# First layer's expert 0 gets its tokens by one-hot products from rows in SBUF instead of an indirect gather, and the slot columns are read one job later

## The chip, the core and the metric

One core of a Trainium2 chip runs the whole kernel as one launch. The metric is the device time of that launch in microseconds (us), the median of several executions. TensorE (PE) multiplies matrices, VectorE (DVE) and ScalarE (ACT) work elementwise, GpSimd (POOL) does elementwise work and issues the indirect DMAs, SyncE (SP) issues most of the weight transfers.

## The reference

Two layers run over 256 latent tokens and 256 context tokens of width 1024. Each layer has a mixer and then a mixture of experts (MoE); only the latent stream is returned, so the second layer's MoE sees 256 tokens and the first layer's sees all 512. What matters here is the MoE and what stands ahead of it:

```python
x_lat = x_lat + g1 * hybrid_mixer(p, u, v, q_a, g, keys, lp, rope_tabs)   # ends with "merged @ w_out"
h2 = modulate(rmsnorm(x_lat, norm2_g[l]), sh2, sc2)                       # h * (1 + scale) + shift
x_lat = x_lat + g2 * moe(h2, router_w, router_b, w_e_gate[l], w_e_up[l], w_e_down[l])
...
# moe(t): 16 experts in 4 groups; best group by its two largest scores, then top 2 experts in it
scores = sigmoid(t @ router_w); sel = scores + router_b
...
for e in range(N_EXPERTS):
    a = silu(t @ w_gate[e]) * (t @ w_up[e])          # 1024 -> 512
    y = y + gate[:, e:e + 1] * (a @ w_down[e])       # 512 -> 1024
```

## The kernel before

**Sparse experts.** Each expert gets a fixed number of slots (64 tokens, for some 64 + 32 or more), cut into *jobs* `(expert, first slot, g)`, with `g = 128 / slots`. With g = 2 a job has 64 slots and the two halves of a 1024-wide row lie on two groups of 64 partitions; with g = 4 it has 32 slots and four groups of 32. The first layer has 25 jobs; job 0 is expert 0's first 64 slots, job 1 its next 32, jobs 2 and 3 the same for expert 1, jobs 4 and 5 are experts 2 and 3. Tokens beyond the slots are handled by a loop at the end of the layer.

**Routing.** Token tile by token tile (t = 0 to 3, 128 tokens each) the output projection ends, `decide(t)` computes the row's rms (`rms`), the router logits (`logit`) and the normalised, modulated rows h2 (`h2_out`), which go to DRAM (`h2d`). At t = 3, `pick` runs a long chain of small DVE operations that ends with the choice `mm_` (1 where a token chose an expert); `first_idx` forms every token's rank within its expert (a prefix sum on TensorE, then `rk`), and `order` counts tokens per expert (`cnt`).

**How a job gets its tokens.** An indirect DMA on POOL (`gather`, issued by `pull_job`) reads the job's rows from h2d by a column of indices into one of three buffers `xgb`. `put_x` transposes them on TensorE and ACT copies the result to `ex`; then the gate and up products (L1614) run. For the experts of fixed rank, 0 and 1 (`fixed` holds their four jobs), the index column is made on the spot by `first_list`: a one-hot of the ranks (DVE, L1159), four one-column matmuls against the token numbers (L1163), and a conversion (L1165). For all others `place` writes a slot list to DRAM with eight indirect DMAs (L1212, index `r_ai`), `fetch` reads it back (`lr`, L1447), and `spread` turns it into columns `sel` and `ixh` (DVE L1454, TensorE L1459, DVE L1462 to L1467). In the second layer the tokens of the fixed experts are already picked another way: `dispatch` multiplies one-hots of the ranks with the h2 rows in SBUF.

**Job order.** In job j TensorE runs gate and up, and in between the previous job's transposes (`hidden`, L1592), its down product (`down`, L1547), the next job's `put_x` (L1383), and for pairs of jobs the sum into the latent rows (`add`, L1581). `sel` is needed from the first `down` on, since it scales the result, so `spread` runs in job 1. `blocks` is a chain of small DVE operations about the overflow loop, in program order after job 1.

**Order of the engines.** Each engine runs its own queue strictly in order, so an instruction that waits holds up all behind it. A scheduler fills the queues from the program's order and estimated times. `warm(n)` puts n matmuls into the TensorE queue whose result nobody reads. Weights stream through eight slots of 2 MB (`wx`); SP issues a slot's next transfer (L1261) when its last reader has ended. POOL issues all indirect DMAs; each takes POOL about 1 us.

## Time and profile before

| | us |
|---|---|
| median of 3 runs | 1330.26 (1328.95 to 1332.95) |
| the profiled execution's own time | 1331.49 |
| its span in the trace | 1329.7 |
| TensorE busy in it | 1228.7 |
| first layer's MoE: starts of the first gate product and of the last down product | 525.57 and 809.84 |

Times in the trace count from the start of the span. The trace lists each f32 matmul as two records, so a count "x16" there stands for 8 matmuls of the program. The mean granted TensorE clock over the span was 0.974 of full speed.

### The profile page before, as it was taken

The page shows a single profiled execution, that of the slowest core. Times are in us where ns is not written, and L with a number is a line of the kernel's source. Part 1 is how long each engine was busy: PE and PEld are TensorE (multiplying, and loading weights), DVE is VectorE, ACT ScalarE, POOL GpSimd, SP SyncE. Part 2 cuts the span into 40 slices and gives each one's busy share as a digit, 9 for nine tenths or more (in the row PEclk, how much of TensorE's full clock was granted, in tenths as well). Part 3 has the DMA queues.
Part 4 walks back from the last instruction along what each step waited for, and adds up shares of the span by engine and source line. Part 5 has one row for each costly group of instructions (what it writes and reads, how often), then busy time and mean ns, then how long its engine had stood idle before and what let it go on. Part 6 is the DMA issues. An engine that isn't in the chain of part 4 may idle for free. (4 is left out here: it accounts for less than half of the span.)

```text
span 1329.7 us, 23222 instructions
## 1 busy us (share of the span) xinstructions
PE 1228.7 (92%) x9376; PEld 830.2 (62%) x9376; DVE 613.0 (46%) x1372; ACT 408.0 (31%) x766; POOL 281.4 (21%) x304
## 2 busy tenths in 40 slices
PE   5899989999999998899999997799999999888985
PEld 2587755656777775555555554688988855555543
DVE  4546545456323554522212234837666854434332
ACT  4434234342222310222212333545554410111111
POOL 0424330002111114212112211544601311100000
PEclk9899989999999997999999998899999999999998
DMA  9421566657564938697999845534343789999993
GB/s 381 156 72 60 191 219 210 207 190 248 180 206 156 355 136 314 243 402 299 417 404 416 327 148 189 204 107 146 118 156 122 276 297 396 421 424 422 425 421 119
DMA packets 70718, 338.48 MB, mean 255 GB/s; under 512 B 9506, under 2 KB 21202, under 8 KB 58064
## 3 DMA queue, kind: packets, MB, share of 16 engines
q1 hardware_dynamic: 59328, 320.93, 64.5%
q0 software_dynamic: 4912, 8.27, 1.8%
q10 hardware_dynamic: 6368, 7.76, 1.6%
q8 instruction: 75, 1.23, 0.4%
q14 instruction: 35, 0.29, 0.1%
HBM read 332.64 MB, written 10.02 MB: 258 GB/s over the span
## 5 line engine op out<-in xcount | busy, mean ns | idle before, releaser
L1614 PE MATMUL mmp<-wx,wh 128*64 128x256 f32 (+1 forms) x3456 | 257.0, 329 | 4.9 <-DVE wh L1528 3.4
L1614 PEld LDWEIGHTS mmp<-wx,wh 128*64 128x64 f32 (+1 forms) x3456 | 161.9, 123 | 92.1 <-issue 40.1
L197 PE MATMUL mmp<-xh,wh 128*128 128x512 f32 (+2 forms) x576 | 209.0, 364 | 8.3 <-ACT xh L421 7.5
L199 PE MATMUL mmp<-xh,wl 128*128 128x512 f32 (+2 forms) x576 | 199.4, 347 | 0.0
L1547 PE MATMUL trp<-wx,r 128*32 128x256 f32 (+1 forms) x944 | 129.1, 480 | 9.5 <-DVE r L1594 9.5
L197 PEld LDWEIGHTS mmp<-xh,wh 128*128 128x128 f32 (+1 forms) x576 | 108.3, 189 | 33.3 <-ACT xh L421 8.0
L199 PEld LDWEIGHTS mmp<-xh,wl 128*128 128x128 f32 (+1 forms) x576 | 108.4, 188 | 18.2 <-issue 2.6
L198 PE MATMUL mmp<-xres,wh 128*128 128x512 f32 (+1 forms) x288 | 114.8, 399 | 0.0
L205 ACT CAST wh<-raw 128x1024 fp32r<-128x1024 f32 (+2 forms) x53 | 54.0, 1024 | 127.3 <-PE mmp L198 47.5
L1547 PEld LDWEIGHTS trp<-wx,r 128*32 128x32 f32 (+1 forms) x944 | 44.6, 122 | 74.3 <-issue 53.5
L198 PE MATMUL mmp<-xl,wh 128*128 128x256 f32 (+2 forms) x288 | 85.1, 296 | 5.3 <-DVE xl L382 5.2
L194 DVE TENSOR_TENSOR wl<-raw,wh 128x1024 fp32r<-128x1024 f32 (+2 forms) x43 | 51.6, 1201 | 82.1 <-ACT wh L205 81.8
L1565 DVE TENSOR_TENSOR wl<-r,wl 64x512 fp32r<-64x512 f32 x54 | 37.1, 686 | 96.7 <-ACT wl L1564 78.6
L205 ACT CAST wh<-wx 128x1024 fp32r<-128x1024 f32 (+2 forms) x55 | 55.9, 1025 | 56.8 <-issue 23.6
L1389 POOL DMA_INDIRECT ysd<-r,ixh x25 | 25.1, 1005 | 199.9 <-ACT r L1556 198.9
L1556 ACT ACTIVATE r<-trp,sel 128x512 f32<-128x512 f32 (+1 forms) x25 | 15.5, 619 | 167.7 <-PE trp L1547 167.7
L198 PEld LDWEIGHTS mmp<-xres,wh 128*128 128x128 f32 (+1 forms) x288 | 54.2, 188 | 15.0 <-issue 1.7
L1641 DVE TENSOR_TENSOR r<-r,mmp 128x256 f32<-128x256 f32 (+1 forms) x43 | 15.9, 370 | 102.4 <-ACT r L1640 102.4
L198 PEld LDWEIGHTS mmp<-xl,wh 128*128 128x128 f32 (+1 forms) x288 | 54.5, 189 | 11.5 <-DVE xl L382 5.9
L194 DVE TENSOR_TENSOR wl<-wx,wh 128x1024 fp32r<-128x1024 f32 (+1 forms) x44 | 56.1, 1283 | 8.1 <-ACT wh L205 8.0
L1581 PE MATMUL atp<-wl 128*128 128x512 f32 (+1 forms) x176 | 48.3, 416 | 11.1 <-ACT wl L1568 7.8
L1346 POOL DMA_INDIRECT wh<-h2d,ixh x24 | 28.2, 1173 | 122.0 <-PE trp L1383 90.8
(388 smaller groups left out, 2075.8 us busy)
## 6 DMA issues: line engine op xcount, KB each, us to landing
wx<-in_wexp_dram SPq DMA_DIRECT2D x79, 2048.0 KB
raw<-in_wmod_dram SPq DMA_DIRECT2D x80, 512.0 KB
wx<-in_wexp_dram SPq DMA_DIRECT2D x44, 512.0 KB
raw<-in_win_dram SPq DMA_DIRECT2D x35, 512.0 KB
wx<-in_win_dram SPq DMA_DIRECT2D x35, 512.0 KB
raws<-in_wmod_dram SPq DMA_DIRECT2D x8, 1024.0 KB
xres<-in_wexp_dram SPq DMA_DIRECT2D x5, 1024.0 KB
trk<-in_wexp_dram SPq DMA_DIRECT2D x5, 1024.0 KB
```

Of the source, the lines that this page charges most:

```text
L194: e.tensor_tensor(dst, full, hi.bitcast(F32), op=OP.subtract)
L197: T.matmul(o, lh, rh, start=first, stop=False, skip_group_check=True)
L198: T.matmul(o, lh, rl, start=False, stop=False, skip_group_check=True)
L199: T.matmul(o, ll, rh, start=False, stop=last_, skip_group_check=True)
L205: S.copy(h[:, :n], src)
L1346: return G.indirect_dma_start(out=xg[:, :D // g], out_offset=None, in_=h2d.rearrange("r (h d) -> (r h) d", h=g), in_offset=bass.IndirectOf ...
L1389: s_i = G.indirect_dma_start(out=ysd.rearrange("r (h d) -> (r h) d", h=g), in_=y, in_offset=None, out_offset=bass.IndirectOffsetOnAxis(ap= ...
L1547: T.matmul(py[i * P // g:(i + 1) * P // g, :w], aT[:, (c % m) * P + c // m * (P // g):(c % m) * P + (c // m + 1) * (P // g)], wcols(wd, o, ...
L1565: V.tensor_tensor(hb[1][rs, cs], y2[rs, :w], yh_.bitcast(F32), op=OP.subtract)
L1581: T.matmul(acc[t][h], one[h][rs, t * P:(t + 1) * P], hb[n][rs, h * 512:(h + 1) * 512], start=(j == 1 and n == 0 and not last), stop=(n == ...
L1614: parts(g, lambda h, gs_: mms.append(T.matmul(px[gs_, i * f:(i + 1) * f], ex[:, (k % n) * P + k // n * q:(k % n) * P + (k // n + 1) * q], ...
L1641: misc["a0"] = V.tensor_tensor(a0[:, :f], a0[:, :f], px[:, f:2 * f], op=OP.mult)
```

## The change

In the first layer the two jobs of expert 0 no longer go through an index column and a gather. All four h2 tiles get SBUF rows of their own (`h2s`), so they stay until the ranks are known. `first_idx` builds one-hots for the two jobs, and `dispatch`, now also for g = 4, multiplies them with the h2 rows into PSUM; DVE copies job 0's result and ACT job 1's to `xgb`. The index columns for expert 1's two jobs move from job 0 into `first_idx`. For the last token tile, h2 is no longer made by ACT and two POOL products but by two DVE operations, the first of them placed right behind the residual sum. The six `warm` matmuls behind `order` go. `spread` and the first two `down` products run in job 2 instead of job 1 (`SPR`), and the gathers for jobs 2 and 3 stand ahead of `place` and of job 0.

```diff
-        h2s = [bcx[:, NR + i, :] for i in range(2)]
+        h2s = [bcx[:, (NR + i) % 4, :] for i in range(NT)]
...
             elif t == NT - 1:
-                S.activation(h2, xres[:, t, :], AF.Copy, scale=rss[:, t:t + 1])
-                G.tensor_tensor(h2, h2, a2b[r], op=OP.mult)
-                G.tensor_tensor(h2, h2, sh2[r], op=OP.add)
+                V.scalar_tensor_tensor(h2, h2, rss[:, t:t + 1], sh2[r], op0=OP.mult, op1=OP.add)
...
-            for n in range(len(fixed) if last else 2):
+            if last:
+                for n in range(len(fixed)):
+                    one_hot(n, hot[:, n])
+                return
+            for n, h in [(n, one_hot(n, r2([P, NT, P // fixed[n][2]]))) for n in range(2)]:
+                dispatch(n, h, 1 - n)
+            for n in range(2, len(fixed)):
                 first_list(n)
-        def dispatch(n):
+        def dispatch(n, h, eng):
+            g = fixed[n][2]
             px = trp()
+            w = D // g
             for t in range(NT):
-                halves(lambda i, gs_: T.matmul(px[gs_], hot[:, n, t], h2s[t][:, i * 512:(i + 1) * 512], start=(t == 0),
-                                               stop=(t == NT - 1), skip_group_check=True))
-            (V.tensor_copy if n == 1 else S.copy)(xgb[n], px)
+                for i in range(g):
+                    T.matmul(px[i * P // g:(i + 1) * P // g, :w], h[:, t], h2s[t][:, i * w:(i + 1) * w], start=(t == 0),
+                             stop=(t == NT - 1), skip_group_check=True)
+            (V.tensor_copy if eng else S.copy)(xgb[n][:, :w], px[:, :w])
...
                 order()
-                if not last:
-                    warm(6)
...
                 res = V.tensor_tensor(x_t[:, hs], x_t[:, hs], tm, op=OP.add)
+                if hf and t == NT - 1 and not last:
+                    V.tensor_tensor(h2s[t], x_t, a2b[r], op=OP.mult)
...
-            for v in range(len(fixed), LA + 2):
+            for v in range(len(fixed), LA + SPR + 1):
                 pull_job(v)
+        SPR = 1 if last else 2
...
-            for j in range(2):
-                tc.keep_in_program_order(pull_job(j))
+            tc.keep_in_program_order(pull_job(2))
         place()
...
-        pend = None
+        pend, downs = None, []
+        if not last:
+            tc.keep_in_program_order(pull_job(3))
...
-                    if i == (j == 1) and pend is not None:
-                        if j == 1:
+                    if j >= SPR and i == (j == SPR):
+                        if j == SPR:
                             spread()
-                        down(pend[0], aT, pend[2])
-                    if i == 0 and j == 0 and not last:
-                        for v in range(2, len(fixed)):
-                            first_list(v)
-                        for v in range(2, min(LA + 1, len(fixed))):
-                            pull_job(v)
+                        while downs:
+                            down(*downs.pop(0))
```

What this does to the queues is seen at three places. TensorE in the first layer, from behind the prefix sum to job 0's gate product, before (L1163 index columns, L1175 counts, L1269 warm, L1383 `put_x`, L1614 gate and up):

```order
L1163 MATMUL trp<-cst,r_4144 128x1 x4
L1163 MATMUL trp<-cst,r_4152 128x1 x4
L1175 MATMUL trp<-r_mm,ones 128x16 x4
L1269 MATMUL mmp<-cst,st_69 128x512 x6
L1383 MATMUL trp<-st_69,wh 128x128 x4
L1163 MATMUL trp<-cst,r_4325 128x1 x4
L1163 MATMUL trp<-cst,r_4333 128x1 x4
L1383 MATMUL trp<-st_69,wh 128x128
L1614 MATMUL mmp<-wx_3689,wh 64x256 x16
```

and now the same stretch (lines renumbered: L1152 `dispatch`, L1173 index columns, L1185 counts, L1394 `put_x`, L1627 gate and up):

```order
L1152 MATMUL trp<-xh,r_4148 64x512 x8
L1152 MATMUL trp<-xh,r_4150 32x256 x16
L1173 MATMUL trp<-cst,r_4181 128x1 x4
L1173 MATMUL trp<-cst,r_4189 128x1 x4
L1185 MATMUL trp<-r_mm,ones 128x16 x4
L1394 MATMUL trp<-st_69,wh 128x128 x6
L1627 MATMUL mmp<-wx_3689,wh 64x256 x16
```

24 `dispatch` matmuls have come in ahead of the counts, the six warm matmuls are gone, and `put_x` of both jobs stands ahead of job 0. The second place is POOL's queue from the end of the routing to the first gather by the slot list, before (L1079 and L1080 the two h2 products, L1346 gathers, L1212 slot list writes, L1447 its read):

```order
L1079 TENSOR_TENSOR xh<-xh,bcy 128x1024
L1080 TENSOR_TENSOR xh<-xh,bcy 128x1024
L1346 DMA wh<-h2d_3613,r_ix_3657 128x512
L1346 DMA wh<-h2d_3613,r_ix_3657 128x256
L1212 DMA lst_3621<-tokid,r_ai 9216x4 x8
L1346 DMA xg<-h2d_3613,r_ix_3657 128x512
L1346 DMA wh<-h2d_3613,r_ix_3657 128x256
L1447 DMA lr_4224<-lst_3621 128x64
L1447 DMA lr_4226<-lst_3621 32x64
```

and now (L1360 gathers, here of jobs 2 and 3, L1222 the writes, L1458 the read):

```order
L1360 DMA xg<-h2d_3613,r_ix_3657 128x512
L1360 DMA wh<-h2d_3613,r_ix_3657 128x256
L1222 DMA lst_3621<-tokid,r_ai 9216x4 x8
L1458 DMA lr_4247<-lst_3621 128x64
L1458 DMA lr_4249<-lst_3621 32x64
```

The products are gone, and nothing stands between the list's writes and its read any more; job 3's gather, which waits for job 0's transposes to leave its buffer, stands ahead of the writes. The third place is DVE between the first silu product and the columns, now (L1650 silu product of jobs 0 and 1, L1605 copy of `hidden`, L1465 and L1466 the conversion of the list, the others `blocks`); before, the conversion L1454 stood right behind job 0's silu product and `blocks` behind the columns:

```order
L1650 TENSOR_TENSOR r_4448<-r_4448,mmp 128x128
L1422 TENSOR_TENSOR r_4452<-r_4452,cst 1x256
L1465 CAST lf_4248<-lr_4247 128x16x2
L1466 COPY lf_4248<-lr_4247 128x16
L1423 TENSOR_REDUCE r_4453<-r_4452 1x16
L1465 CAST lf_4250<-lr_4249 32x16x2
L1466 COPY lf_4250<-lr_4249 32x16
L1424 TENSOR_TENSOR r_ov<-r_cnt,r_4453 1x16
```

Here `blocks` stands behind the conversion and ahead of L1605, the copy that job 1's `down` and the PSUM slot of `spread` need.

## Rows read from the trace of the kernel before

**Rows 1.** The page: TensorE's busy time (part 1) and DMA share (part 2).

```profile
PE 1228.7 (92%) x9376; PEld 830.2 (62%) x9376; DVE 613.0 (46%) x1372; ACT 408.0 (31%) x766; POOL 281.4 (21%) x304
...
DMA  9421566657564938697999845534343789999993
```

**Rows 2.** TensorE timeline from the routing to job 0 (start, length, what, count, idle before).

```profile
498.96 5.22 PE L1269 MATMUL mmp<-cst,st 128*128 128x512 f32 x8
...
509.87 3.54 PE L1163 MATMUL trp<-cst,r 128*128 128x1 f32 x16 [1.13 <-DVE r L1159]
513.28 1.87 PE L1175 MATMUL trp<-r_mm,ones 128*128 128x16 f32 x8
514.99 7.52 PE L1269 MATMUL mmp<-cst,st 128*128 128x512 f32 x12
522.35 0.60 PE L1383 MATMUL trp<-st,wh 128*128 128x128 f32 x4
522.78 0.95 PE L1163 MATMUL trp<-cst,r 128*128 128x1 f32 x8
...
525.57 7.09 PE L1614 MATMUL mmp<-wx,wh 128*64 128x256 f32 x48
```

**Rows 3.** Busy time by stretch; the third number from the end is the granted clock.

```profile
502.30:509.00 6.70, 2.92 (x13) 1.54 (x11) 5.28 (x27) 0.63 (x1) 0.00 (x0) 1.00 1.04 396
509.10:519.30 10.20, 9.43 (x29) 6.97 (x30) 5.75 (x22) 0.00 (x0) 2.43 (x2) 0.50 0.70 243
```

**Rows 4.** DVE timeline of the routing and the list's index.

```profile
489.92 1.28 DVE L1082 SCALAR_TENSOR_TENSOR xh<-xres,r_rss,bcy 128x1024 f32<-128x1024 f32 x1 [0.66 <-POOL r_rss L1070]
...
492.38 0.23 DVE L1065 SCALAR_TENSOR_TENSOR r_lgs<-r_lgs,r_rss,r_cr 128x16 f32<-128x16 f32 x1
...
497.59 1.55 DVE L1065 SCALAR_TENSOR_TENSOR r_lgs<-r_lgs,r_rss,r_cr 128x16 f32<-128x16 f32 x1
499.47 2.12 DVE L1106 TENSOR_SCALAR r_sco<-r_sco 128x64 f32<-128x64 f32 x1 [0.32 <-ACT r_sco L1105]
...
507.33 0.23 DVE L1127 TENSOR_TENSOR r_mm<-r_ohs 128x64 f32<-128x64 f32 x1
...
515.18 0.17 DVE L1176 COPY r_cnt<-trp 128x16 f32<-128x16 f32 x1 [1.49 <-PE trp L1175]
...
519.79 0.15 DVE L1209 TENSOR_SCALAR r_ai<-r_af 128x8 int32<-128x8 f32 x1
```

**Rows 5.** POOL timeline: an h2 product, first list write, read of the list.

```profile
496.77 2.34 POOL L1079 TENSOR_TENSOR xh<-xh,bcy 128x1024 f32<-128x1024 f32 x1 [1.26 <-ACT xh L1078]
...
520.22 1.21 POOL L1212 DMA_INDIRECT lst<-tokid,r_ai  x1 [3.37 <-DVE r_ai L1209]
...
534.99 1.14 POOL L1447 DMA_DIRECT2D lr<-lst  x2 [1.95 <-DMA lst<-tokid,r_ai]
```

**Rows 6.** DVE timeline: conversion of the list, then the ends of a piece of `blocks`.

```profile
537.37 0.17 DVE L1454 CAST lf<-lr 128x32 f32<-128x32 int32 x1
...
549.23 0.41 DVE L1412 TENSOR_REDUCE r<-r 1x16 f32<-1x256 f32 x1
...
554.53 0.41 DVE L1426 TENSOR_REDUCE r<-r 1x16 f32<-1x256 f32 x1
```

**Rows 7.** TensorE timeline within the jobs.

```profile
541.13 1.10 PE L1459 MATMUL trp<-lf,st 128*64 128x45 f32 x32
...
555.29 1.93 PE L1547 MATMUL trp<-wx,r 128*32 128x256 f32 x32 [2.15 <-DVE r L1594]
...
558.07 1.50 PE L1614 MATMUL mmp<-wx,wh 128*32 128x128 f32 x42 [0.48 <-ACT wh L1521]
...
581.68 1.95 PE L1614 MATMUL mmp<-wx,wh 128*64 128x256 f32 x16
...
597.30 3.60 PE L1547 MATMUL trp<-wx,r 128*64 128x512 f32 x16
```

**Rows 8.** The longest of SP's waits from 530 to 760 us (total, times, longest).

```profile
SPq L1261 <- PE mmp L1614: 121.4, 22, 19.6
```

More of the change, by code (lines that the diff above doesn't have):

```diff
@@ L1073, in h2_out @@
             r = t // 2
-            h2 = h2s[t % 2]
+            h2 = h2s[t]
             if last:
@@ L1138, in first_idx, with one_hot @@
                                    op1=OP.mult)
-            for n in range(len(fixed) if last else 2):
+            if last:
[5 more added lines that the diff above has]
+            for n in range(2, len(fixed)):
                 first_list(n)
-        def dispatch(n):
+        def dispatch(n, h, eng):
+            g = fixed[n][2]
             px = trp()
+            w = D // g
             for t in range(NT):
-                halves(lambda i, gs_: T.matmul(px[gs_], hot[:, n, t], h2s[t][:, i * 512:(i + 1) * 512], start=(t == 0),
-                                               stop=(t == NT - 1), skip_group_check=True))
-            (V.tensor_copy if n == 1 else S.copy)(xgb[n], px)
+                for i in range(g):
+                    T.matmul(px[i * P // g:(i + 1) * P // g, :w], h[:, t], h2s[t][:, i * w:(i + 1) * w], start=(t == 0),
+                             stop=(t == NT - 1), skip_group_check=True)
+            (V.tensor_copy if eng else S.copy)(xgb[n][:, :w], px[:, :w])
+        def one_hot(n, h):
+            p, s0, g = fixed[n]
+            w = P // g
+            q = [P, NT, w]
+            ready.append(V.tensor_tensor(h, C("i256")[:, None, s0 + 1:s0 + w + 1].to_broadcast(q),
+                                         rk[:, :, p:p + 1].to_broadcast(q), op=OP.is_equal))
+            return h
         def first_list(n):
             p, s0, g = fixed[n]
-            if last:
-                q = [P, NT, 64]
-                ready.append(V.tensor_tensor(hot[:, n], C("i256")[:, None, s0 + 1:s0 + 65].to_broadcast(q),
-                                             rk[:, :, p:p + 1].to_broadcast(q), op=OP.is_equal))
-                return
             pi = trp()
@@ L1339, in trunk @@
                     pends.append(lambda t=t: decide(t))
+        wkb = [[wk.tile([P, 1024], F32R, name=nm, bufs=3) for _ in range(3)] for nm in ("wh", "wl")]
+        fb = [v.bitcast(F32) for v in wkb[0]]
+        hb = wkb[1]
+        xgb = [fb[0][:, :512], fb[0][:, 512:]]
         pends.pop(0)()
@@ L1357, in trunk @@
         mo = pm_.enter_context(tc.tile_pool(name=f"mo{l}", bufs=1, reuse_waits="tile"))
-        wkb = [[wk.tile([P, 1024], F32R, name=nm, bufs=3) for _ in range(3)] for nm in ("wh", "wl")]
-        fb = [v.bitcast(F32) for v in wkb[0]]
-        hb = wkb[1]
         xgp = mo.tile([P, 1024], F32, name="xg")
-        xgb = [fb[0][:, :512], fb[0][:, 512:], xgp[:, :512]]
-        for xg in () if last else xgb:
+        xgb.append(xgp[:, :512])
+        for xg in () if last else (xgb[2], xgb[1][:, 256:]):
             with tc.issue_after(ready[0].ins):
-                S.activation(xg.rearrange("p (a b) -> p a b", b=P), ones[:, None, :].to_broadcast([P, 4, P]),
+                S.activation(xg.rearrange("p (a b) -> p a b", b=P), ones[:, None, :].to_broadcast([P, xg.shape[1] // P, P]),
                              AF.Copy, scale=0.0)
@@ L1497, in trunk @@
             for n in range(3):
-                dispatch(n)
+                dispatch(n, hot[:, n], n == 1)
         else:
-            for j in range(2):
-                tc.keep_in_program_order(pull_job(j))
+            tc.keep_in_program_order(pull_job(2))
         place()
@@ L1604, in trunk @@
             nx, fin = xs(j + 1) if j + 1 < len(jobs) else (None, None)
-            if j > 1 or j == 1 and jobs[1 + LA][0] < nst:
+            if j > SPR:
                 pull_job(j + LA)
@@ L1620, in trunk @@
                         if (i, k) == (0, 3) and pend is not None:
[L1621 removed]
+                            downs.append((pend[0], hidden(*pend[:2]), pend[2]))
                         if (i, k) == (1, 3) and fin:
                             fin()
[L1624 to L1625 removed]
+                    if j >= SPR and i == (j == SPR):
+                        if j == SPR:
                             spread()
[L1627 to L1632 removed]
+                        while downs:
+                            down(*downs.pop(0))
             if j == 0:
```

1 line of the change is left out of this document (removed).

## The prediction

> **What bounds the kernel now.** I read the page first: TensorE is busy 92% of the span and the DMA share is at its ceiling in much of the first layer's MoE [rows 1], so the question is which of the two sets the pace there, and what happens in the stretch before it. The waits of SP's queue say that between 530 and 760 us a weight transfer mostly starts when a gate or up product lets its slot go [rows 8]: the weights follow TensorE. The TensorE timeline of the same stretch shows one product behind the other, with idle time only near 555 and 558 us [rows 7]. So the MoE lasts as long as TensorE's work in it, and its end is set by when that work begins: 525.57 us [rows 2].
>
> Then the timeline ahead of that. The choice of experts ends on DVE at 507.33 + 0.23 = 507.56 [rows 4]. From there to the first gate product 18.0 us pass, in which TensorE does little that is of use: two index lists (3.54), the counts (1.87), warm matmuls (7.52), transposes and two more lists [rows 2]. From 509.1 to 519.3 its granted clock is 0.50, the 1.2 GHz level, after a stretch in which it was busy for only 2.92 of 6.70 us [rows 3].
>
> **The change, step by step.**
>
> *1. The choice.* POOL's two h2 products run from 496.77, each about 2.34 us [rows 5]. In that time DVE's L1065 takes 1.55 us where a row of the same shape takes 0.23, and L1106 takes 2.12, where a DVE operation on 128x64 takes 0.23 [rows 4]. With POOL's products gone I take back 1.32 + 1.89 = 3.2 us. DVE gets two operations of 1.28 us instead [rows 4]. The first lies while DVE waits for ACT's square sum, the second before the last logits are there (L1065 begins at 497.59). I price them at 0; if the second stands wholly in the way, 1.3. The choice then ends at 504.3 (to 505.6).
>
> *2. Start of the products.* Before, 2.31 us lie between the choice and the first list product at 509.87 (prefix sum, ranks, a one-hot of 512 columns). The one-hot now has 256 columns; I take 2.1, start 506.4. The first five warm matmuls end at 498.96 + 5.22 = 504.18 [rows 2], so the 3 us of idleness behind them all but vanish.
>
> *3. `dispatch`.* The trace has no such product in the first layer, but two down products have exactly their shapes: 8 matmuls of 64 columns by 512 took 3.60 us, 16 of 32 by 256 took 1.93 [rows 7]. At that clock the sum is 5.5, end 511.9; at half of it 11.1. I take the full clock, since TensorE is now busy from 498.96 on with no gap near the one that went before the fall in [rows 3]. Job 0's copy on DVE runs beside the second product.
>
> *4. Lists and counts.* The two lists of expert 1 now stand here: 0.95 each at full clock, 3.54 together at half [rows 2]. The counts took 1.87 at half; at full I scale to 1.0. So 513.8, then 514.8.
>
> One rule speaks of the lists. The Trainium skill, "TensorEngine Tiling (Array Packing)", section Instruction Overhead, says that a matmul of one column costs as much as one of 60, about 60 cycles. At 2.4 GHz that would be an estimated 0.4 us for 16 such records instead of the measured 1.9, and the lead 1.5 larger; the rows go against it, and I go by the rows.
>
> *5. Warm matmuls and `put_x`.* 7.52 us of warm matmuls go. Transposes 0.60 and ACT's copy of the same length lie on the path: job 0 starts at 516.0, a lead of 9.5. Were the clock half from 506.4 on: 506.4 + 11.1 + 3.5 + 1.9 + 1.2 + 0.6 = 524.7, a lead of 0.9.
>
> *6. The list.* It is needed one job later but depends on the counts, which come only 0.4 earlier than before (514.8 against about 515.15). From the counts to the index took 515.18 to 519.94 [rows 4]; one list one-hot no longer lies between, so I take 4.3: index at 519.2, first write 519.5 (before 520.22). From the first write to DVE's conversion of the list 17.15 us passed (520.22 to 537.37) [rows 5, 6]. The read waited for the writes to land, not for the two gathers in between, so I keep 17.1: list at 536.6. Job 3's gather, which now stands ahead of the writes, waits for job 0's transposes (515.4) and is done before the index.
>
> *7. Job 0 to job 3.* Job 0 took 7.09 for 48 records of 64, part of them at the low clock [rows 2]; with the rest at 0.122 each it is 9.0. Job 1: 128 records at 1.50/42 and 0.9 of transposes, 5.5. Job 2: 4 x 1.95 and 0.5, 8.3 [rows 7]. `spread` is thus due at 538.8. But DVE's `blocks` stands between the list and the copy L1605 whose PSUM slot `spread` takes over. That piece lasted 5.7 us (549.23 to 554.94) with a few other operations in it [rows 6]; alone I take 5.0. So `spread` starts at 541.6 and TensorE waits 2.8. With 1.10 for `spread` and 3.60 + 1.93 for the two down products [rows 7], job 3 starts at 548.2, against 558.07 [rows 7]: the lead is 9.9. What TensorE loses here, it also lost before (2.15 at 555.29, 0.48 at 558.07).
>
> *8. From job 3 on.* The order of the jobs' work is the same. Slots come free 9 to 10 us sooner, and the transfers with them; gathers for jobs 4 and 5 follow `spread` as before. I carry the 9.9 to the end unchanged, as the second layer's queues keep their order.
>
> **Sum.** 1331.49 for the profiled execution less 9.9 gives 1321.6. The median of the runs stands 1.23 below that execution, so 1320.4; I say 1320.5.
>
> **The rivals.**
>
> *A. The clock stays low.* It fell at 509.1 with little done before it, and lists and counts did not lift it [rows 3]. If it falls at the choice, `dispatch` costs twice: counts at 522.9, list at 544.7, `spread` at 549.7, job 3 at 556.3, lead 1.8: 1328.5. If only half of `dispatch` is hit, the lead is about 6: 1324.3. The Trainium skill, "TensorE: Matmul & The Clock Gate", section on HAM oscillation, says that pauses between bursts of matmuls put the engine back to its lower level. The fall in [rows 3] agrees. [...] Against it: the pause that came before that fall is the one that step 2 closes.
>
> *B. The weights hold the pace.* The DMA share is at the ceiling for several slices [rows 1]. If the transfers could not come sooner, job 0 would start earlier and wait later: no change, 1330.3. Against it: SP's waits are for TensorE, not the other way [rows 8].
>
> *C. The list comes late (slower).* All that stands behind the list's conversion on DVE (L1605, so job 1's down product, `spread`, the columns) waits for it, and with the two down products the slot of expert 0's third weight. Job 3 starts 11.6 us after the list, so the change turns to a loss if the list lands after 546.5, which is 9.9 later than I have it. For it: the first weight slots come free about 10 us sooner, so 2 MB transfers now run beside the list's last writes and its read. If these took 34 instead of 17.1 us, the list would land at 553.5, a loss of 7.0: 1337.3. Against it: the writes ran beside weight transfers before as well.
>
> *D. No wait at `spread`.* If `blocks` or the list are quicker than in steps 6 and 7, TensorE runs on: job 3 at 545.4, lead 12.7, 1317.6.
>
> **How the numbers follow.** Steps 1 to 8 as they stand with leads of 8 to 12, 0.56; D 0.07; A in part 0.15, A in full 0.09; B 0.06; C 0.07. The range goes from D less 0.6 for the unknowns of step 1 and the tail, 1317.0, up to 1327.5, which cuts into A in full; it leaves out B, C and most of A in full. A run of this kernel can tell about 0.3% from no change, 4 us. Faster: steps, D and A in part, 0.78. Same: A in full and B, 0.15. Slower: C, 0.07.
>
> **What would show it.** Right, if L1104, the old L1106, takes about 0.2; if `dispatch` takes about 5.5 us with the clock at 1.00; if the first L1627 starts near 516 and the first L1627 of job 3 near 548 with a wait for DVE of some us at L1470; and if all later rows lie 9 to 10 us earlier. Wrong, if the clock is 0.50 in 506 to 512, if the conversion L1465 starts well behind 537, or if products in 560 to 720 begin to wait for weights.

## The result: 0.6% slower, where 0.7% faster was forecast

| | before | after |
|---|---|---|
| median (10 runs each), us | 1331.59 (1327.68 to 1336.57) | 1338.72 (1334.72 to 1342.08) |
| ratio to before | | 1.0056 [1.0042, 1.0069] |
| profiled execution's own time, us | 1331.49 | 1338.63 |
| its span, us | 1329.7 | 1336.8 |
| its mean granted TensorE clock | 0.974 | 0.970 |

The same kernel, run again twice beside later experiments, gave 1.0039 [1.0023, 1.0055] and 1.0029 [1.0009, 1.0049]. So the sign is sure; the three estimates of the size lie between 0.3 and 0.6%.

One correction comes ahead of all comparisons of rows. The two profiled executions differ by 2.04 us before anything that the change touches: the last sum of the residual ahead of the routing starts at 493.24 us before, at 495.29 after (first row below). "From the common point" means a start less this one. In the profiles of all kernels below it lies between 492.5 and 496.0 us.

DVE's timeline after, the rows that answer to [rows 4] and [rows 6] (start, length, engine, line, operation, tiles, count, idle time before and what ended it):

```profile
495.29 0.69 DVE L1337 TENSOR_TENSOR xres<-xres,r 128x512 f32<-128x512 f32 x1
...
499.95 0.20 DVE L1104 TENSOR_SCALAR r_sco<-r_sco 128x64 f32<-128x64 f32 x1 [0.34 <-ACT r_sco L1103]
505.87 0.22 DVE L1125 TENSOR_TENSOR r_mm<-r_ohs 128x64 f32<-128x64 f32 x1
...
543.53 0.18 DVE L1465 CAST lf<-lr 128x32 f32<-128x32 int32 x1 [10.71 <-DMA lr<-lst]
...
544.80 0.17 DVE L1465 CAST lf<-lr 32x32 f32<-32x32 int32 x1 [0.70 <-DMA lr<-lst]
...
545.36 1.14 DVE L1427 SCALAR_TENSOR_TENSOR r_nb<-r_ov,r_nb 1x16 f32<-1x16 f32 x6
...
548.57 0.27 DVE L1605 COPY r<-trp 128x128 f32<-128x128 f32 x1
```

The small operations of the routing cost 0.20 us instead of 2.12, and the choice ends 3.5 us earlier from the common point. But the list (L1465) is converted at 543.5 and 544.8 us, and behind it stands `blocks` (the rows with `r_nb` and their like), 3.8 us from the second conversion, until L1605.

TensorE's timeline after, from `dispatch` to job 3 (answers to [rows 2] and the first rows of [rows 7]):

```profile
508.10 5.52 PE L1152 MATMUL trp<-xh,r 128*64 128x512 f32 x48 [0.82 <-PE trp L1133]
513.55 1.05 PE L1173 MATMUL trp<-cst,r 128*128 128x1 f32 x8
514.85 1.05 PE L1173 MATMUL trp<-cst,r 128*128 128x1 f32 x8 [0.25 <-DVE r_ix L1175]
515.77 1.04 PE L1185 MATMUL trp<-r_mm,ones 128*128 128x16 f32 x8
...
517.97 2.28 PE L1627 MATMUL mmp<-wx,wh 128*64 128x256 f32 x10 [0.46 <-ACT wh L1532]
...
537.88 1.95 PE L1627 MATMUL mmp<-wx,wh 128*64 128x256 f32 x16
548.89 1.51 PE L1470 MATMUL trp<-lf,st 128*64 128x45 f32 x32 [9.07 <-DVE r L1605]
550.33 8.16 PE L1558 MATMUL trp<-wx,r 128*64 128x512 f32 x48
558.31 2.78 PE L1627 MATMUL mmp<-wx,wh 128*32 128x128 f32 x90
...
562.47 2.09 PE L1592 MATMUL atp<-wl 128*128 128x512 f32 x8 [1.38 <-DVE wl L1581]
```

Up to job 2 the forecast stands: job 0 starts at 517.97 (9.6 earlier from the common point) and job 2 ends at 539.83. Then TensorE waits 9.07 us for DVE at `spread`, and the work behind the wait is slow: `spread` 1.51 instead of 1.10, the down products 8.16 instead of 3.60 + 1.93 [rows 7]. Job 3 starts at 558.31, 1.8 earlier from the common point instead of 9.9.

Why the list was late, in three views. POOL's timeline after (first write of the list, its read; before in [rows 5]):

```profile
521.33 1.01 POOL L1222 DMA_INDIRECT lst<-tokid,r_ai  x1 [2.81 <-DVE r_ai L1219]
...
537.21 1.15 POOL L1458 DMA_DIRECT2D lr<-lst  x2 [5.93 <-DMA lst<-tokid,r_ai]
```

SP's timeline after, two 2 MB transfers of expert weights, into the slots that jobs 0 and 1 have set free:

```profile
528.73 0.33 SPq L1271 DMA_DIRECT2D wx<-in_wexp_dram  x1
...
531.89 0.34 SPq L1271 DMA_DIRECT2D wx<-in_wexp_dram  x1
```

The same two before:

```profile
538.10 0.33 SPq L1261 DMA_DIRECT2D wx<-in_wexp_dram  x1
...
541.26 0.34 SPq L1261 DMA_DIRECT2D wx<-in_wexp_dram  x1
```

From first write to conversion 22.2 us pass (521.33 to 543.53), before 17.15 [rows 5, 6]; the read alone takes 543.53 - 537.21 = 6.3 us, before 537.37 - 534.99 = 2.4. So 3.9 of the 5.1 us are the read's, the rest the writes'. The two figures of before are upper bounds: there DVE did not wait for the list, but converted it right behind the silu product of job 0, which ended at 537.45. DVE's timeline before:

```profile
537.03 0.42 DVE L1641 TENSOR_TENSOR r<-r,mmp 128x256 f32<-128x256 f32 x1 [11.79 <-ACT r L1640]
```

Before, the two transfers went out when the list was already there; now they go out while it is written and read. (Expert 2's first two weights, issued from about 520 us on in both kernels, run beside the writes before as well.) Busy time by stretch after (PE, PEld, DVE, ACT, POOL, then granted clock, DMA share and GB/s):

```profile
533.00:538.00 5.00, 5.00 (x45) 2.87 (x43) 0.00 (x0) 0.00 (x0) 0.79 (x2) 1.00 1.05 434
...
542.00:555.70 13.70, 6.81 (x46) 2.86 (x48) 8.21 (x48) 0.00 (x0) 1.88 (x2) 0.50 0.28 111
```

and before, while the list was read:

```profile
533.00:537.40 4.40, 3.84 (x64) 2.44 (x66) 0.37 (x2) 2.04 (x3) 1.18 (x3) 1.00 0.23 81
```

While the list is read, the DMA share is 1.05 where before it was 0.23. And from 542.0 to 555.7 TensorE's clock is at 0.50, its 1.2 GHz level, after it had been idle from 539.83 on: that is the slow work behind the wait, 0.41 + 2.63 = 3.0 us of it.

The end of the layer also differs. TensorE's timeline after, from the last job's transposes to the last sums into the latent rows:

```profile
797.92 0.44 PE L1394 MATMUL trp<-st,wh 128*128 128x128 f32 x2
798.29 1.95 PE L1627 MATMUL mmp<-wx,wh 128*64 128x256 f32 x16
801.18 0.44 PE L1603 MATMUL trp<-st,r 128*128 128x128 f32 x2 [0.94 <-DVE r L1650]
802.18 3.65 PE L1558 MATMUL trp<-wx,r 128*64 128x512 f32 x16 [0.56 <-issue]
...
810.29 1.95 PE L1627 MATMUL mmp<-wx,wh 128*32 128x128 f32 x64
812.97 0.33 PE L1603 MATMUL trp<-st,r 128*128 128x128 f32 x1 [0.72 <-DVE r L1650]
...
819.01 2.07 PE L1592 MATMUL atp<-wl 64*128 64x512 f32 x4 [0.62 <-ACT wl L1579]
```

and before:

```profile
796.26 0.44 PE L1383 MATMUL trp<-st,wh 128*128 128x128 f32 x2
796.63 2.94 PE L1614 MATMUL mmp<-wx,wh 128*64 128x256 f32 x42
799.52 0.44 PE L1592 MATMUL trp<-st,r 128*128 128x128 f32 x2
...
800.66 3.65 PE L1547 MATMUL trp<-wx,r 128*64 128x512 f32 x16
804.25 2.17 PE L1614 MATMUL mmp<-wx,wh 128*32 128x128 f32 x70
...
814.26 2.24 PE L1581 MATMUL atp<-wl 64*128 64x512 f32 x8 [2.48 <-ACT wl L1568]
```

Before, job 23's transposes (799.52) and down product stand in between products of job 24. After, they stand ahead of all of them, and TensorE waits 0.94, 0.56 and 0.72 us for what those products had covered. The same work takes 819.01 + 2.07 - 797.92 = 23.2 us, before 816.50 - 796.26 = 20.2. The scheduler set this order; no line of the diff touches job 24.

From the common point the lead is thus 9.6 us at job 0, 1.8 at job 3, 0.4 near 720 us (1.2 of this loss is the wait at L1592, 1.38 instead of 0.22, for the weights of the first sum, which DVE makes from `sel`), and -2.5 at the layer's last sums. Behind these another 2.5 us come together: from the end of the last sums to the end of the span 515.8 us pass, before 513.2. In the two other profiles of the changed kernel (runs 7 and 13 below) it is 515.2 and 515.6, in the two profiles of another kernel (runs 1 and 17) 512.2 and 515.3, and of the kernel before there is one profile alone. So it is not shown whether these 2.5 us belong to the change, and nothing here gives them a cause.

### The profile page after: what moved, and what is told of

Its sections match the earlier page's. It is cut to its first block, busy times and chain, and to the rows that moved or that the text cites. A ratio compares the mean times of both kernels' runs of the same rounds, so it can differ in the third digit from the quotient of the medians.

```text
span 1336.8 us, 23248 instructions
## 1 busy us (share of the span) xinstructions
PE 1229.0 (92%) x9396; PEld 828.4 (62%) x9396; DVE 612.7 (46%) x1373; ACT 405.9 (30%) x765; POOL 272.7 (20%) x300
## 5 line engine op out<-in xcount | busy, mean ns | idle before, releaser
L1627 PE MATMUL mmp<-wx,wh 128*64 128x256 f32 (+1 forms) x3456 | 255.2, 329 | 4.0 <-DVE wh L1539 3.4
L1627 PEld LDWEIGHTS mmp<-wx,wh 128*64 128x64 f32 (+1 forms) x3456 | 161.8, 123 | 88.6 <-issue 36.9
L1558 PE MATMUL trp<-wx,r 128*32 128x256 f32 (+1 forms) x944 | 132.0, 486 | 8.0 <-DVE r L1605 7.3
L1592 PE MATMUL atp<-wl 128*128 128x512 f32 (+1 forms) x176 | 49.7, 422 | 12.2 <-ACT wl L1579 7.2
L1650 DVE TENSOR_TENSOR r<-r,mmp 128x256 f32<-128x256 f32 (+1 forms) x43 | 15.9, 370 | 92.1 <-ACT r L1649 92.0
L1360 POOL DMA_INDIRECT wh<-h2d,ixh x24 | 27.6, 1152 | 128.8 <-PE trp L1394 100.2
## 6 DMA issues: line engine op xcount, KB each, us to landing
raws<-in_wmod_dram SPq DMA_DIRECT2D x8, 1024.0 KB, 11.4
```

The costliest lines, as they stand in the source:

```text
L1360: return G.indirect_dma_start(out=xg[:, :D // g], out_offset=None, in_=h2d.rearrange("r (h d) -> (r h) d", h=g), in_offset=bass.IndirectOf ...
L1558: T.matmul(py[i * P // g:(i + 1) * P // g, :w], aT[:, (c % m) * P + c // m * (P // g):(c % m) * P + (c // m + 1) * (P // g)], wcols(wd, o, ...
L1592: T.matmul(acc[t][h], one[h][rs, t * P:(t + 1) * P], hb[n][rs, h * 512:(h + 1) * 512], start=(j == 1 and n == 0 and not last), stop=(n == ...
L1627: parts(g, lambda h, gs_: mms.append(T.matmul(px[gs_, i * f:(i + 1) * f], ex[:, (k % n) * P + k // n * q:(k % n) * P + (k // n + 1) * q], ...
L1650: misc["a0"] = V.tensor_tensor(a0[:, :f], a0[:, :f], px[:, f:2 * f], op=OP.mult)
```

## The experiments

Three theories. **T1**: the list comes late because the two 2 MB transfers run beside its writes and its read (rival C). **T2**: `blocks` ahead of L1605 holds `spread`. **T3**: the new order at the layer's end costs 3 us. A fourth, on steps in TensorE's own work, came up with the first runs. All ratios are to the kernel before, run beside each.

| run | edit | median, us | ratio [95%] |
|---|---|---|---|
| e1 | two weight transfers held until the list is there | 1331.77 | 1.0004 [0.9990, 1.0018] |
| e2 | ten warm matmuls ahead of `spread` | 1338.58 | 1.0053 [1.0034, 1.0071] |
| e3 | old order at the layer's end | 1333.64 | 1.0012 [0.9996, 1.0029] |
| e4 | `blocks` in job 4 | 1335.06 | 1.0023 [1.0007, 1.0038] |
| e5 | four transfers held | 1335.85 | 1.0032 [1.0018, 1.0046] |
| e6 | four held, `blocks`, end | 1336.23 | 1.0025 [1.0008, 1.0041] |
| e7 | none | 1337.81 | 1.0039 [1.0023, 1.0055] |
| e8 | kernel before with the new end | 1334.16 | 1.0024 [1.0010, 1.0038] |
| e9 | two held, `blocks`, end | 1322.77 | 0.9945 [0.9923, 0.9966] |
| e10 | e9 and four warm matmuls before job 1 | 1325.86 | 0.9953 [0.9933, 0.9972] |
| e11 | `spread` back in job 1 | 1340.90 | 1.0070 [1.0046, 1.0094] |
| e12 | the six warm matmuls back | 1332.59 | 1.0014 [0.9997, 1.0030] |
| e13 | none | 1334.07 | 1.0029 [1.0009, 1.0049] |
| e14 | `blocks`, end | 1330.81 | 1.0005 [0.9988, 1.0022] |
| e15 | e9 again | 1323.32 | 0.9941 [0.9918, 0.9965] |
| e16 | e6 again | 1324.59 | 0.9962 [0.9942, 0.9982] |
| e17 | e1 again | 1330.63 | 1.0000 [0.9983, 1.0017] |
| e18 | two held, `blocks` | 1326.85 | 0.9972 [0.9951, 0.9992] |

Runs 1 to 4, 5 to 8, 9 to 12, 13 to 16, and 17 and 18 ran together, each group a batch with its own runs of the kernel before. The changed kernel itself ran beside the kernel before in the result's measurement and as runs 7 and 13; elsewhere a contrast with it goes by way of the kernel before. From the three it is 7.1, 6.4 and 4.3 us slower.

**The four edits.** Holding: a DVE copy of one element of the list into the weight slot, which the transfer must wait for.

```diff
-        def wexp(e, i, eng=None, pin=True, parts=1):
+        def wexp(e, i, eng=None, pin=True, parts=1, hold=None):
...
+            if hold is not None:
+                with tc.issue_after(misc["lf"].ins):
+                    V.tensor_copy(w[0][0:1, 0:1], hold[0:1, 0, 0:1])
...
-                    V.tensor_copy(f[:n, :, 2], raw_[:n, :, 3].bitcast(F32))
+                    misc["lf"] = V.tensor_copy(f[:n, :, 2], raw_[:n, :, 3].bitcast(F32))
...
+            if not last:
+                for q_ in ((2, 2), (3, 0)):
+                    early[q_] = wexp(*q_, hold=lsr[-1][0])
```

Runs 5, 6 and 16 hold `(2, 0)` and `(2, 1)` too, which then go out whole and no longer early in four parts. `blocks` later, and the old order at the end:

```diff
-            if j == 1:
+            if j == (1 if last else 4):
                 blocks()
...
-                            downs.append((pend[0], hidden(*pend[:2]), pend[2]))
+                            with tc.issue_after(mms[-1].ins) if j == len(jobs) - 1 else ExitStack():
+                                downs.append((pend[0], hidden(*pend[:2]), pend[2]))
...
-                            down(*downs.pop(0))
+                            with tc.issue_after(mms[-1].ins) if j == len(jobs) - 1 else ExitStack():
+                                down(*downs.pop(0))
...
-            if j >= len(jobs) - LATE:
+            if j >= len(jobs) - LATE and (last or j != len(jobs) - 2):
```

Warm matmuls into the wait (run 2; nobody reads them):

```diff
                         if j == SPR:
+                            if not last:
+                                warm(10)
                             spread()
```

**Runs 1 to 4.** Expected of run 1:

> The changed kernel with one thing added: the 2 MB transfers of expert 2's third part and expert 3's first part, which in the changed kernel are issued at 528.7 and 531.9 us, wait until the list has landed (two one-element DVE copies behind the conversion). Theory 1, these transfers stand ahead of the list's read: the read takes about 2 us instead of 6.3, from the first list write to the first conversion pass 17 to 18 us instead of 22.2, the wait of TensorE at spread falls from 9.1 to 4 or less, its clock stays up, and job 3 starts 5 to 8 us earlier; time 1331 to 1334 instead of 1338.7. Rival, the list's own writes are slow or the DVE chain behind the conversion is what counts: the conversion stays 22 us behind the first write, 1338 to 1340.

Of run 2:

> The changed kernel with ten matmuls that nobody reads between job 2 and spread, about 8.5 us at full clock, to fill the wait. In it the scheduler also puts the last products of the layer back in the order of the kernel before. Theory 2, the wait also costs the clock of what follows: spread still starts near 548.9 but spread and the two down products take about 6.6 instead of 9.7 us, job 3 starts 3 us earlier; with the tail's order another 1 to 2 us; 1333.5 to 1336. Rival, the clock would have come back by itself or the filling delays spread: 1337 to 1340.

Of run 3:

> The changed kernel with the last job's gate product again ahead of the transposes and the down product of the job before it, as the scheduler had it in the kernel before. Theory 3, part of the loss is the order of the last job: from the last up product to the end of the layer's sums 2 to 3 us less, of which at least 1 us reaches the end: 1335.5 to 1337.7. Rival, the next layer waits for something else there (its weights, the sums' rows from DRAM): no change, 1338 to 1339.5.

Of run 4:

> The changed kernel with the chain of small DVE operations about the overflow loop (blocks) behind job 4 instead of job 1, so that nothing but the conversion stands between the list and the copy that spread waits for. If the list is late as in the changed kernel, spread starts 0.5 instead of 4 us behind the second conversion, job 3 about 3.5 to 4.5 us earlier (the columns behind spread come sooner too): 1333.5 to 1335.5. Rival, what is won is lost to waits behind it, since the gathers of jobs 4 to 6 and the weights set the pace there: 1337.5 to 1339.5.

Against the kernel before, run 1 is level, run 3 1.9 us slower, run 4 3.3 and run 2 6.8. Set against the changed kernel's 4.3 to 7.1, run 1 gave back 4 to 7 us, run 3 2 to 5, run 4 1 to 4, and run 2 nothing that can be told. But the profiles of these runs show a thing that the profile after does not: in job 1 TensorE stops several times with nothing to wait for that the profile shows. In run 3 the order at the end is the old one again, and the stretch of 23.2 us takes 20.7; that part of T3 stands. In run 2 the warm matmuls took 8.85 us in front of `spread`, which began only at 554.18, so the rival of its expectation, that the filling delays `spread`, came true; whether the warm matmuls save the clock can't be read from it.

**Runs 5 to 8.** Is it the transfers that make TensorE stop, and how much does the end cost alone? In run 8 the kernel before gets the new end:

```diff
+                if not last and j == len(jobs) - 1:
+                    es.enter_context(tc.issue_after(misc["dn"].ins))
...
+                    if i == 0 and not last and j == len(jobs) - 1:
+                        adds.pop(0)()
+                        es.enter_context(tc.issue_after(misc["ad"].ins))
```

(with the last down and sum instructions kept in `misc`).

> The changed kernel with four weight parts held until the list has landed: expert 2's first two, which the changed kernel issues from 522 us on and which fill the DMA queues while jobs 0 and 1 run, and the two 2 MB transfers held in e1_weights_after_list. In four of five profiles of kernels with the change TensorE falls into single steps in job 1, with 3 to 4 us of gaps in which it waits for nothing that the trace shows, and then into its lower clock, while these transfers run. Theory 4, the transfers beside job 1 starve TensorE's instruction stream: without them no such gaps, jobs 0 to 2 take 22 us instead of 29, the list's conversion comes about 17 us behind the first write, and job 3 starts 6 to 9 us earlier than in e1_weights_after_list: 1324 to 1328. Rival 1, the gaps come from something in the program and stay: 1331 to 1333, as e1_weights_after_list. Rival 2, the weights then come too late for job 4 and the products wait for them: slower than e1_weights_after_list.

> All three edits in one: the four weight parts held until the list has landed, blocks behind job 4, and the last job's gate product ahead of the transposes of the job before. If the three causes are separate and each is what theory 1, 3 and 4 say, nothing is left between the predicted steps and the end: job 3 starts about 10 us earlier than in the kernel before, 1319 to 1323, faster than both. Rival, the gain in the middle is lost at the layer's end or in the second layer: 1326 to 1331.

> The changed kernel once more, unaltered, for a second profile beside the same runs of the kernel before. If the steps of TensorE in job 1 are the usual case and the first profile the exception, they are here again: 3 to 4 us of gaps in job 1, jobs 0 to 2 in 29 instead of 22 us, spread with no wait near 548.8; if the first profile was the usual case, a wait of about 9 us at spread with the low clock behind it. The time is 1337 to 1340 by either.

> The kernel before with one thing of the changed kernel: the last job of the first layer in the order that the scheduler gave the changed kernel (transposes, down product and sums ahead of the two halves of its products). Theory 3: the layer's sums end 2 to 3 us later and the run is 1.5 to 5 us slower than before, 1333 to 1337. Rival, the order of the last job is covered by what the next layer waits for: 1331 to 1332.

Run 8 shows T3 from the other side: the kernel before becomes 0.24% slower, 2.7 us, with the new end alone. In its profile, which is of its fastest run, the stretch takes 21.8 us. In runs 5 to 7 the stops are there again. TensorE's timeline of run 7, the unaltered changed kernel, in job 1:

```profile
531.28 0.41 PE L1627 MATMUL mmp<-wx,wh 128*32 128x128 f32 x4 [1.04 <-issue]
...
545.67 1.95 PE L1627 MATMUL mmp<-wx,wh 128*64 128x256 f32 x16
547.48 1.10 PE L1470 MATMUL trp<-lf,st 128*64 128x45 f32 x32
548.51 5.52 PE L1558 MATMUL trp<-wx,r 128*64 128x512 f32 x48
```

The stops sum to 3.4 us, and products behind them run at half speed; job 2 ends at 547.6 instead of 539.8, so `spread` has nothing to wait for, and holding transfers and moving `blocks` have little to give. That fits run 6, which gained only 1.6 us on run 7. My fourth theory, that the transfers stop TensorE, falls with run 5: with four transfers held the DMA share in its job 1 is 0.03, and the stops are still there:

```profile
520.00:534.00 14.00, 10.69 (x84) 6.12 (x84) 2.38 (x10) 1.33 (x2) 7.83 (x9) 0.86 0.03 4
```

**Runs 9 to 12.** Only two transfers held, with the other edits; then the same with warm matmuls (`warm(4)` between jobs 0 and 1) against the stops; `spread` back in job 1 (`SPR = 1`), the slot columns' old place; and the six warm matmuls back behind `order()`.

> The edits of e1_weights_after_list, e4_blocks_later and e3_tail_order in one; expert 2's first two parts go out early again, unlike e6_all_three. If holding all four parts is what cost e6_all_three its gain (job 20 came 2.4 us later against job 8 than in the other profiles), this one is at least as good as the best of the three: 1328 to 1331.5. If the steps of TensorE in job 1 set the pace whatever the list does, it stays with e1_weights_after_list: 1331 to 1333.

> e9_two_held_blocks_tail with four matmuls that nobody reads between job 0 and job 1, 3.4 us at full clock. Holding all weights did not take the steps in job 1 away, so it is not the weights that make them; if TensorE's own stream of short products runs ahead of what feeds it, a few long ones before it let that catch up: no gaps in job 1, clock at 1.00 through jobs 1 and 2, spread 2 to 4 us earlier than in e9_two_held_blocks_tail: 1326 to 1330. Rival, the steps stay and the four matmuls come on top: 3 us slower than e9_two_held_blocks_tail.

> The changed kernel with one part undone: spread and the first down product in job 1 again, as in the kernel before. If the list is late, TensorE waits for it at the end of job 1 with the work of job 2 still to do: spread near 545, job 3 at 560 or later, the same as the changed kernel or slower: 1338 to 1342. Rival, the move of spread is itself what costs: 1331 to 1334.

> The changed kernel with one part undone: the six warm matmuls behind order are back, so job 0 starts about 5 us later. With them the scheduler also puts the last job in the order of the kernel before. If the lead of job 0 is worth nothing because the list and the steps in job 1 eat it, nothing is lost: no steps in job 1 (the long matmuls stand ahead of it), spread still at 547 to 550, and with the old tail 1333 to 1335. Rival, the lead is worth its length: 1341 to 1344.

Run 9 is 0.55% faster than the kernel before. None of these four profiles shows the stops. TensorE's timeline of run 9 (L1633 gate and up, L1473 `spread`, L1564 `down`, L1598 the sums):

```profile
539.60 1.95 PE L1633 MATMUL mmp<-wx,wh 128*64 128x256 f32 x16
541.38 1.05 PE L1473 MATMUL trp<-lf,st 128*64 128x45 f32 x32
542.36 5.52 PE L1564 MATMUL trp<-wx,r 128*64 128x512 f32 x48
547.70 2.78 PE L1633 MATMUL mmp<-wx,wh 128*32 128x128 f32 x90
...
788.21 0.44 PE L1397 MATMUL trp<-st,wh 128*128 128x128 f32 x2
...
807.07 2.07 PE L1598 MATMUL atp<-wl 64*128 64x512 f32 x4 [0.62 <-ACT wl L1585]
```

and POOL's of the same (first write, read):

```profile
522.01 1.02 POOL L1222 DMA_INDIRECT lst<-tokid,r_ai  x1 [2.73 <-DVE r_ai L1219]
...
537.19 1.15 POOL L1461 DMA_DIRECT2D lr<-lst  x2 [5.24 <-DMA lst<-tokid,r_ai]
```

The list is converted at 539.25: 17.24 us behind the first write and 2.06 behind the read, about as in the kernel before. `spread` waits for nothing, the products behind it run at full speed, and the end takes 20.9 us. From the common point job 3 leads by 12.5 us, the last sums by 9.5, the span by 10.0.

Run 10's warm matmuls (3.70 us) came back as a later job 0 to 2 and gave nothing. Run 11 speaks for the move of `spread` by a job: in job 1 it waits 11.70 us for the list, and the kernel is 10.3 us slower than before, against 4.3 to 7.1; the intervals of run 11 and of the result overlap. In run 12 job 0 starts 7 us later than in the changed kernel, and yet the run is not slower but 2 to 5 us faster than that (2.0 behind the kernel before, against 4.3 to 7.1): `spread` begins at 548.24, as in the changed kernel, because the list sets it (its read took 6.2 us here too), with a wait of 2.33 instead of 9.07; and the end has the old order again. So while the list is late, the early start of job 0 is worth nothing that these runs show.

**Runs 13 to 18.** With no stops in any of these profiles, the edits could be taken one by one.

> The changed kernel unaltered, as the base of this batch. If the steps in job 1 go with the batch, they are in all four profiles here or in none; if they go with the kernel, they are here and in e16_all_three_again and not in e15_e9_again. The time is 1336 to 1340 by either.

> e9_two_held_blocks_tail without its hold: the transfers of expert 2's third part and expert 3's first part stand ahead of the list's read again. If they are what makes the list late, its read takes about 6 us again, spread waits and starts 3 to 5 us later than in e15_e9_again: 1326 to 1330. If blocks and the tail's order are all that matters: 1321 to 1324, as e15_e9_again.

> e9_two_held_blocks_tail once more: without the steps in job 1, 1321 to 1324; with them about 7 us of its gain are lost, 1328 to 1331.

> e6_all_three once more: four parts held instead of two, all else as e15_e9_again. If the later weights cost 2.4 us between jobs 8 and 20 and nothing else differs, 2 to 4 us slower than e15_e9_again; if the steps in job 1 were the rest, the gap to e15_e9_again is that small in this batch too.

> e1_weights_after_list once more: two transfers held, blocks and the tail as in the changed kernel. Without the steps in job 1 this is the situation that the prediction assumed (list about 17 us behind the first write, blocks between list and spread): a wait of 2 to 3.5 us at spread, job 3 near 551, 1324 to 1328. With the steps in job 1: 1331 to 1333 as before.

> Two transfers held and blocks behind job 4, the tail in the order that the scheduler gave the changed kernel. If the tail's order costs 2 to 3 us by itself, 1325 to 1327, between e17_hold_alone_again and e9_two_held_blocks_tail, with no wait at spread; if it costs nothing, 1322 to 1324.

Run 17, the hold alone, brings the time to that of before; `blocks` moved as well (run 18) takes off another 3.8 us, the end (runs 9 and 15) another 3 to 4. From the changed kernel's three measurements, 4.3 to 7.1 us slower than before, the hold alone is thus worth 4 to 7. Within one batch, run 14 and run 15 have the two other edits without the hold and with it: 1330.81 against 1323.32, 7.5 us. Without the hold these two edits (run 14) leave the wait. TensorE's timeline of run 14, then of run 17:

```profile
545.77 1.51 PE L1470 MATMUL trp<-lf,st 128*64 128x45 f32 x32 [5.39 <-DVE r L1605]
547.21 8.06 PE L1558 MATMUL trp<-wx,r 128*64 128x512 f32 x48
```

```profile
542.53 1.10 PE L1473 MATMUL trp<-lf,st 128*64 128x45 f32 x32 [3.12 <-DVE r L1611]
543.55 7.21 PE L1564 MATMUL trp<-wx,r 128*64 128x512 f32 x48
550.59 2.78 PE L1633 MATMUL mmp<-wx,wh 128*32 128x128 f32 x90
```

In run 14 the read takes 6.50 us, in run 17 1.99. Run 14's wait is shorter than the 8.92 of run 13 by about `blocks`. In run 17 `blocks` makes the wait of 3.12 that step 7 had foreseen (2.8), the down products behind it take 7.21 us instead of 5.52, and with the list on time job 3 leads by 7.0. At the last sums run 17 leads by 2.7, and its time is level with the kernel before.

Run 16 holds four transfers. Its list is converted earliest (535.20), 13.5 us behind its first write: with a DMA share of 0.03 the read begins 11.4 us behind that write, before 14.8. Job 3 leads as in run 9, but the lead shrinks from 12.5 at job 3 to 7.1 near 720 us, where the DMA share is 1.0 and its products take longer; that the weights come late there is argued, since the profile names no wait for them. In the end it is 1.3 us slower than run 15. Why it gained nothing as run 6 and 5 us as run 16 I put down to the stops in the former: from the common point its first sum begins 9.3 us later than run 16's, 7.3 of it in jobs 0 to 2.

Several of the measured times missed what was expected. Runs 5 and 6 were slower than the theory had them, with the stops; runs 3 and 9 were faster than their ranges. The changed kernel as run 13 came 1.9 us under its range, and run 17 2.6 us above the one that it had without stops, though its wait was as expected.

## Why the prediction was wrong, step by step

- **Steps 1 to 5 hold in the first profile, but step 3 not as a rule.** There the choice came 3.5 us earlier (3.2 forecast), `dispatch` took 5.52 (5.5) at the full clock, lists and counts 1.05, 1.05 and 1.04, and job 0 led by 9.6 (9.5). The rule on one-column matmuls (the Trainium skill, "TensorEngine Tiling (Array Packing)", section Instruction Overhead), by which eight records would take an estimated 0.2 us, does not agree with the 1.05 measured. In that time the weight loads that go with the eight records were busy for 0.97 us. But rival A came true in part: in run 13, the same kernel, the clock is at 0.50 in `dispatch`, which takes 7.2 us (the second row gives a stretch within it), and job 0 leads by 7.3. Of the 18 profiles of kernels with the change, 9 show 5.5 us there and 9 from 7.2 to 8.0. That the first profile showed the full clock was luck. Run 13's rows:

```profile
506.22 7.21 PE L1152 MATMUL trp<-xh,r 128*64 128x512 f32 x48 [0.82 <-PE trp L1133]
```

```profile
507.00:510.00 3.00, 3.00 (x10) 1.20 (x8) 0.61 (x2) 0.00 (x0) 0.00 (x0) 0.51 1.04 399
```

- **Step 6 failed, at "so I keep 17.1".** It took 22.2. For the read I kept a duration from a stretch in which the DMA engines had little to do, after having worked out myself, in rival C, that the weights would move into it. Runs 9 and 17 show that with the two transfers out of the way the whole is 17.24 and 16.75. The writes were not undisturbed before either: with four transfers held (run 16) the whole is 13.5.
- **Step 7 was right on `blocks`, and failed on what a wait costs.** With the list on time the wait is 3.12 (2.8 forecast), and without `blocks` none (run 18). With the list late it is 9.07, and I had priced the products behind it at the full clock: 3.0 us more for `spread` and the down products at half speed. With the list on time (run 17) it is still 1.7 us.
- **Step 8 failed, at "The order of the jobs' work is the same".** I had looked at the order of the stretch that changed, not at that of job 24. The end costs 2.9 us in the profile, 2.7 in run 8 (1.5 in its profile), 3 to 4 between run 18 and runs 9 and 15. There is a smaller miss too: the 1.2 us at the first sum, which no run takes away.
- **Rival C was the right mechanism** with too small a chance, 0.07, and too high a point of loss: I had the change lose from a list at 546.5 on. The list landed at 543.5 (541.5 counted from the common point as before), and the kernel was slower, since the clock and the end took what was left. That its price, 1337.3, lies near the measured 1338.72 is luck: it assumed 34 us where 22.2 passed. Its counter-argument, that the writes ran beside transfers before as well, spoke of the writes; the read had not.
- **The sum** of 9.9 became -2.5 at the layer's last sums. Up to job 3 it lost 8.1, about the sum of a wait 6.3 longer than forecast and 3.0 by the clock, while jobs 0 to 2 were 0.9 shorter than forecast and job 0 began 0.1 earlier. From job 3 to 720 us it lost 1.4 and at the end 2.9. No run has these misses undone and all else as forecast. In run 9, where the last sums lead by 9.5, `blocks` is moved too, so that the wait counted in step 7 is gone; its lead of 12.5 at job 3 is rival D's case (12.7), and 3.0 of it is lost behind. That 9.5 lies near 9.9 is thus no proof of the sum.
- **What stays open** is the rest up to the medians. The changed kernel is 2.5 us behind at the last sums and 4.3 to 7.1 in time; run 9 leads by 9.5 there and gains 7.8, run 15 by 9.4 and gains 6.4, run 17 by 2.7 and gains nothing. So some us more are lost than the layer shows against the one profile of the kernel before. Step 8 had carried the lead to the end unchanged; whether that failed in the second layer too, or whether that one profile is a favourable one, is not shown.

What isn't settled is why the scheduler changed the order of job 24. Its estimated times end earlier in the changed kernel, and putting back the six warm matmuls (run 12) brought the old order back; I take the estimates to be the cause, but this is argued only.

## What to carry to other kernels

When work moves earlier, ask what it sets free and what that starts: here the freed weight slots sent 4 MB into the very stretch in which a small list was still being written and then read, and holding two transfers back until it was there gave back 4 to 7 us. A duration taken from a quiet stretch is no price for a busy one, and a wait costs more than its length when the clock falls in it. And take more than one profile of a kernel before a step is called confirmed: `dispatch` took 5.5 us in half of them and over 7 in the others. After a change, compare the order of work far from it too, here of the last job: a scheduler that works by estimated times may have moved it.

## What the runs showed of the hardware

- **A small read behind large transfers.** The list's read, 40 KB in two pieces, took 2.0 to 2.1 us (runs 9, 15, 17, 18; at most 2.4 before) and 5.8 to 6.5 us (after, runs 12, 13, 14) with two 2 MB transfers on their way from another engine's queue. From the first of the eight list writes to the read 11.4 us passed with a DMA share of 0.03 (run 16), 14.8 before and 15.9 after. The Trainium skill, "DMA: Bandwidth & Descriptors", section Issuing engines are not separate DMA queues, says that the transfers of all engines end up on the same 16 DMA engines and interleave there; this case agrees.
- **The clock after a wait.** After the change it was at its 1.2 GHz level from 542.0 to 555.7 us; TensorE was idle from 539.8 to 548.9 and busy for 6.8 us of that stretch. In run 17, with 3.12 us of idleness, the down products took 7.21 us instead of 5.52, at a granted clock of 0.80 from 542.5 to 551.0.
- **Stops of TensorE without a cause in the profile.** In runs 1 to 7 job 1's 128-column products show four to seven gaps put down to issue, 3.4 to 4.4 us in all, and a stretch at half clock with them or behind; in the profile after and in runs 9 to 18 there are none. The kernels of runs 7 and 13, 6 and 16, 1 and 17 are the same, so the same kernel shows them in one batch of runs and not in another. The kernel matters as well: run 8, without the change, ran beside runs 5 to 7 and shows a single gap of 0.34 us ahead of job 1, the kernel before one of 0.48. The transfers do not make it (run 5). What does stays open; a contrast of a few us that rests on one batch may be misread because of it.
